# One low-part subtraction in four moved from VectorE to GpSimd in the experts' weight splits

## The chip, the cores and the metric

The program runs on one core of a Trainium2 chip. The metric is the device time of one execution in microseconds (us), the median of several runs. The engines are named as in the profile: PE is TensorE (PEld its weight loads), ACT is ScalarE, DVE is VectorE, POOL is GpSimd, SP is SyncE, which here only issues transfers.

## The reference

Three transformer blocks run one after another on 512 tokens of width 1024, all in float32. The change touches only the last part of the third block, a mixture of 32 experts. Cut to what matters:

```python
def hierarchical_moe(x, w_group, b_group, w_expert, b_expert, w_gate, w_up, w_down):
    # each token: best of 4 groups, then the best 2 of that group's 8 experts
    ...
    def run_block(args):
        xblk, e = args                       # up to 128 tokens of expert e
        hid = jax.nn.silu(xblk @ w_gate[e]) * (xblk @ w_up[e])
        return hid @ w_down[e]
    yb = lax.map(run_block, (xb, block_expert)).reshape(cap, d)
    y = yb * slot_w[:, None]
    ... # summed per token
```

`w_gate` and `w_up` are 1024x512 and `w_down` is 512x1024 for each expert, 2 MB each in float32.

## The kernel before

Every float32 product is made of three matmuls in the faster fp32r format. A weight tile `raw` is split in two: `h`, the value rounded to fp32r, and `l = raw - h`, the low part, rounded as well. With the activations split in the same way, the product is (high x high) + (high x low weight) + (low x high weight). The split is one ACT instruction (`copy`, profile line L184) and one DVE instruction (`tensor_sub`, L185), both of 128x1024 elements in the expert stage.

The expert stage is the last 600 us or so of the program. Each expert has 12 weight pieces of 128x1024 elements (512 KB): four of gate, four of up, four of down. SP loads them far ahead into 13 rotating `ew` buffers and, for every second expert, into the tiles `B` (gate), `hH` (up) and `A` (down). `splits` (from L1882) takes one piece, allocates a high and a low tile from two pools of three buffers each (`wh`, `wl`), and issues the cast and the subtraction. A piece then feeds six PE matmuls of 128x512: L2045 to L2047 for gate and up, L2073 to L2075 for down; the second of each three (L2046, L2074) is the one that reads `wl`. With three buffers the cast of a piece cannot start until PE has finished with the piece three places ahead of it.

The stages follow one another on PE in the order up(e+1), gate(e+2), down(e+1), up(e+2) and so on, four pieces each. Between them stand the transposes of the gathered tokens and of the hidden activations (L208), whose results `px` are split into `hL` or `dHL` by ACT and DVE again (L184, L185, 128x512). DVE also multiplies gate and up (L2062). POOL's queue holds two indirect transfers per expert: the gather of an expert's tokens (L2053, `C<-dr,itok`), which waits for PE's transposes of the tokens that the buffer held, and the scatter with addition of its result (L2078, `dr<-C,itok`), which waits for ACT's scaled copies of the result (L2077). Each engine executes its queue in order; the queues are laid out by a scheduler when the program is built. A loop for experts with more than 128 tokens stands behind the 32 experts.

Of the kernel before, what the change touches and what calls it, by code (L numbers as in the profile page):

```python
# [1300 lines left out]
def block3(K, out):  # L1301
    nc, tc, a = K.nc, K.tc, K.a
# [522 lines left out]
    def esrc(e):  # L1825
        return list(epieces(wG[e], wU[e], wD[e]))
# [3 lines left out]
    def eload(src, raw=None):  # L1830
        if raw is None:
            raw = ep.tile([P, 2, S], F32, name=K.nm("ew"), tag="ew")
        nc.sync.dma_start(raw, src)
        return raw
# [44 lines left out]
    for j, b in enumerate([st_[:, j] for j in range(4)] + [brow(), brow()]):  # L1879
        pre.append(eload(esrc(2)[j], b.rearrange("p (k n) -> p k n", k=2)))  # L1880

    def splits(raw):  # L1882
        h = K.wh.tile([P, 2, S], F32R, name=K.nm("wh"), tag="wh")
        l = K.wl.tile([P, 2, S], F32R, name=K.nm("wl"), tag="wl")
        K.split(h, l, raw)
        return h, l


    with ExitStack() as ctx:
# [9 lines left out]
        with ExitStack() as c2:  # L1899
# [106 lines left out]
            with tc.issue_after(last.ins):  # L2006
                for k in range(3):
                    pre[k] = splits(pre[k])
# [72 lines left out]
        def parts_of(pieces, ready=(), bufs=()):  # L2081
            ready, pieces, bufs = list(ready), list(pieces)[len(ready):], list(bufs)

            def nxt():
                r = ready.pop(0) if ready else eload(pieces.pop(0), bufs.pop(0) if bufs else None)
                return r if isinstance(r, tuple) else splits(r)

            return nxt
# [66 lines left out]
def whole(tc, a, out):  # L2155
    with ExitStack() as ctx:
        K_ = K(tc, ctx, a)
        block1(K_)
        block2(K_)
        block3(K_, out)  # L2160
# [32 lines left out]
```

## Time and profile before

| | |
|---|---|
| median of 3 runs | 2992.31 us (2991.24 to 2999.27) |
| the profiled execution: its time | 2999.19 us |
| its span, first to last instruction | 2997.3 us |
| PE busy over the span | 2883.6 us (96%) |
| DVE busy | 1754.3 us (59%) |
| ACT busy | 1410.7 us (47%) |
| POOL busy | 160.6 us (5%) |

Shares over the whole span mix stages with different limits. For this change only the stage from about 2340 us to 2965 us counts, and in it the question is which engine another one waits for, not which is busy. The stage repeats almost to the nanosecond from expert to expert: the scatter starts at 2521.97 us and the next at 2540.80 us, so one expert takes 18.83 us.

### The profile page before, as it was taken

To read this page: it belongs to the slowest core of one execution; us is meant where nothing else is said; L and a number is where in the kernel's file an instruction comes from. 1 tells how busy PE (TensorE), PEld (TensorE's weight loads), DVE (VectorE), ACT (ScalarE), POOL (GpSimd) and SP (SyncE) were. 2 spreads that over 40 slices of the span, in tenths; PEclk is the share of its full clock that TensorE was granted. 3 is DMA by queue.
4 is the path that set the end of the run, shared out by engine and by line. 5 is a ranking of instruction groups with operands and counts; after the bars stand their busy time and mean duration, and the time that the engine had idled before them with its cause. 6 is when DMAs were issued, how large, how long until landed. Compare 5 with 4: busy or idle time off the path is not lost.

```text
span 2997.3 us, 38485 instructions
## 1 busy us (share of the span) xinstructions
PE 2883.6 (96%) x14652; PEld 2377.1 (79%) x14652; DVE 1754.3 (59%) x2815; ACT 1410.7 (47%) x2297; POOL 160.6 (5%) x145
## 2 busy tenths in 40 slices
PE   8999999999999999999999999999999799999995
PEld 7788878888788878778888889888877577777774
DVE  4544453344675675645333363766554788888886
ACT  4422333333354455532222223656343488888885
POOL 0000000000000000000000000000000111111111
PEclk9999999999999999899999999999999799999998
DMA  5233333333422221133333343112433899999984
GB/s 174 90 93 92 96 95 98 99 98 94 122 70 56 66 57 47 46 120 99 99 99 95 105 132 115 29 36 73 157 117 144 292 318 347 338 344 365 353 309 141
DMA packets 330693, 428.42 MB, mean 143 GB/s; under 512 B 34381, under 2 KB 240904, under 8 KB 330506
## 3 DMA queue, kind: packets, MB, share of 16 engines
q1 hardware_dynamic: 320714, 415.41, 42.2%
q0 software_dynamic: 9792, 10.53, 1.6%
q8 instruction: 116, 1.90, 0.3%
q14 instruction: 71, 0.58, 0.1%
HBM read 420.60 MB, written 30.41 MB: 150 GB/s over the span
## 4 chain that ended last, share of the span: by engine, by line
PE 70%; issue 14%; DMA 8%; DVE 4%; ACT 2%; POOL 1%; POOLq 0%; SPq 0%; DVEq 0%; ACTq 0%
PE pf L267 28%; DMA dr<-C,itok 7%; PE pc L310 5%; PE pc L311 5%; PE pc L309 5%; PE pf L342 2%; PE pf L343 2%; PE pf L344 2%; PE pnO L1554 1%; PE pg L1650 1%; PE phO L1140 1%; PE pf L179 1%; PE pf L180 1%; PE pf L181 1%; PE pnS L179 1%
## 5 line engine op out<-in xcount | busy, mean ns | idle before, releaser
L159 DVE TENSOR_TENSOR wl<-raw,wh 128x1024 fp32r<-128x1024 f32 (+2 forms) x322 | 391.2, 1215 | 686.0 <-ACT wh L158 682.8
L158 ACT CAST wh<-raw 128x1024 fp32r<-128x1024 f32 (+2 forms) x322 | 336.3, 1045 | 865.1 <-PE pf L267 365.3
L267 PE MATMUL pf<-hL,wh 128*128 128x512 f32 x1272 | 501.7, 394 | 0.0
L267 PE MATMUL pf<-hH,wh 128*128 128x512 f32 x1208 | 478.2, 396 | 0.0
L267 PE MATMUL pf<-hH,wl 128*128 128x512 f32 x1208 | 476.1, 394 | 0.0
L267 PEld LDWEIGHTS pf<-hL,wh 128*128 128x128 f32 x1272 | 239.4, 188 | 51.2 <-issue 3.7
L267 PEld LDWEIGHTS pf<-hH,wh 128*128 128x128 f32 x1208 | 227.6, 188 | 52.3 <-issue 4.6
L267 PEld LDWEIGHTS pf<-hH,wl 128*128 128x128 f32 x1208 | 227.3, 188 | 48.8 <-issue 2.6
L185 DVE TENSOR_TENSOR wl<-ew,wh 128x1024 fp32r<-128x1024 f32 x186 | 225.9, 1223 | 34.0 <-ACT wh L184 29.8
L184 ACT CAST wh<-ew 128x1024 fp32r<-128x1024 f32 x186 | 194.2, 1053 | 48.5 <-PE pc L2047 31.0
L2046 PE MATMUL pc<-wl,hL 128*128 128x512 f32 x512 | 204.8, 400 | 0.5 <-DVE wl L185 0.4
L2047 PE MATMUL pc<-wh,hL 128*128 128x512 f32 x512 | 204.5, 400 | 0.0
L2045 PE MATMUL pc<-wh,hL 128*128 128x512 f32 x512 | 204.0, 399 | 0.0
L192 POOL TENSOR_TENSOR s<-s,mhalf 128x1 f32<-128x1 f32 (+1 forms) x69 | 57.8, 838 | 2253.3 <-DVE s L190 2244.6
L342 PE MATMUL pf<-wh,hH 128*128 128x256 f32 (+2 forms) x576 | 164.3, 286 | 0.0
L343 PE MATMUL pf<-wl,hH 128*128 128x256 f32 (+2 forms) x576 | 163.0, 283 | 0.0
L309 PE MATMUL pc<-wh,B 128*128 128x512 f32 x416 | 162.9, 392 | 0.0
L310 PE MATMUL pc<-wl,B 128*128 128x512 f32 x416 | 162.8, 391 | 0.0
L344 PE MATMUL pf<-wh,hL 128*128 128x256 f32 (+2 forms) x576 | 162.2, 282 | 0.0
L311 PE MATMUL pc<-wh,C 128*128 128x512 f32 x320 | 124.6, 389 | 0.0
L2046 PEld LDWEIGHTS pc<-wl,hL 128*128 128x128 f32 x512 | 96.3, 188 | 27.7 <-DVE wl L185 3.0
L2073 PE MATMUL pc<-wh,dHL 128*128 128x512 f32 x256 | 103.3, 404 | 11.1 <-ACT dHL L184 11.1
(695 smaller groups left out, 5932.3 us busy)
## 6 DMA issues: line engine op xcount, KB each, us to landing
raw<-w_in SPq DMA_DIRECT2D x111, 512.0 KB, 3.9
raw<-w_ff SPq DMA_DIRECT2D x64, 512.0 KB, 3.8
ew<-moe_w_down SPq DMA_DIRECT2D x64, 512.0 KB, 9.4
B<-moe_w_gate SPq DMA_DIRECT2D x64, 512.0 KB, 6.6
hH<-moe_w_up SPq DMA_DIRECT2D x64, 512.0 KB, 6.6
A<-moe_w_down SPq DMA_DIRECT2D x64, 512.0 KB, 6.3
ew<-moe_w_up SPq DMA_DIRECT2D x62, 512.0 KB, 5.5
ew<-moe_w_gate SPq DMA_DIRECT2D x60, 512.0 KB, 6.6
```

Of the source, the lines that this page charges most:

```text
L158: nc.scalar.copy(h, raw)
L159: nc.vector.tensor_sub(l, raw, h)
L185: self.nc.vector.tensor_sub(l, src, h)
L267: self.nc.tensor.matmul(ps[:n, sl], u[:, k], v[:, sl], start=(k == 0 and i == 0 and sl.start == 0), stop=(k == nk - 1 and i == 2), skip_gr ...
L309: mm(pss[t][:, :n], ah[:, ts], wh[:, k], start=(kg == 0), stop=False)
L310: mm(pss[t][:, :n], ah[:, ts], wl[:, k], start=False, stop=False)
L311: mm(pss[t][:, :n], al[:, ts], wh[:, k], start=False, stop=(kg == nk - 1))
L342: mm(o[t], ah[:, ts], wh[:, k], start=st, stop=False, skip_group_check=True)
L343: mm(o[t], ah[:, ts], wl[:, k], start=False, stop=False, skip_group_check=True)
L344: mm(o[t], al[:, ts], wh[:, k], start=False, stop=(kg == nk - 1), skip_group_check=True)
L2046: mm(ps, aH[:, kg], l[:, k], start=False, stop=False)
L2047: mm(ps, aL[:, kg], h[:, k], start=False, stop=(kg == n - 1))
```

## The change

The split of an expert's weight piece is written out in `splits`, with a counter. The cast stays on ACT. The subtraction of every fourth piece is issued to GpSimd instead of VectorE:

```diff
+    nsp = [0]
+
+
     def splits(raw):
+        nsp[0] += 1
         h = K.wh.tile([P, 2, S], F32R, name=K.nm("wh"), tag="wh")
         l = K.wl.tile([P, 2, S], F32R, name=K.nm("wl"), tag="wl")
-        K.split(h, l, raw)
+        nc.scalar.copy(h, raw)
+        (nc.vector if nsp[0] % 4 else nc.gpsimd).tensor_sub(l, raw, h)
         return h, l
```

Since each of gate, up and down has four pieces, it is always the fourth piece of each. Below L1881 the line numbers grow by five: L2046 becomes L2051, L2053 becomes L2058, L2078 becomes L2083, and the subtractions of the pieces stand at L1890.

On POOL, at the start of the expert stage, the queue before held three memsets, the gathers and the scatters:

```order
L1898 MEMSET C_18688 128x1024 x2
L1914 MEMSET C_18688 128x128
L2053 DMA C_18688<-dr_18207,itok 128x1024 x4
L2078 DMA dr_13402<-C_18688,itok 512x1024
L2053 DMA C_18688<-dr_18207,itok 128x1024
```

Now the subtractions stand among them:

```order
L1903 MEMSET C_18688 128x1024 x2
L1919 MEMSET C_18688 128x128
L2058 DMA C_18688<-dr_18207,itok 128x1024 x3
L1890 TENSOR_TENSOR wl_18865<-ew_18273,wh_18864 128x1024
L1890 TENSOR_TENSOR wl_18908<-ew_18341,wh_18907 128x1024
L2058 DMA C_18688<-dr_18207,itok 128x1024
L1890 TENSOR_TENSOR wl_18967<-B_18659,wh_18966 128x1024
L1890 TENSOR_TENSOR wl_19019<-ew_18421,wh_19018 128x1024
L2083 DMA dr_13402<-C_18688,itok 512x1024
L1890 TENSOR_TENSOR wl_19065<-hH_18664,wh_19064 128x1024
L2058 DMA C_18688<-dr_18207,itok 128x1024
```

From the last scatter on, the pattern repeats for each expert: scatter, the fourth up piece, a gather, the fourth gate piece, the fourth down piece, the next scatter. POOL gains 99 such instructions, three of them in the loop behind the experts.

On DVE, in the repeating part, with an even expert's up and down in `ew` and the next expert's gate in `B`, the queue before was:

```order
L185 TENSOR_TENSOR wl_19564<-ew_19561,wh_19563 128x1024
L185 TENSOR_TENSOR wl_19576<-ew_19573,wh_19575 128x1024
L185 TENSOR_TENSOR wl_19606<-B_18659,wh_19605 128x1024
L185 TENSOR_TENSOR wl_19617<-B_18659,wh_19616 128x1024
L2062 TENSOR_TENSOR scr_19475<-scr_19475,pc_19536 128x512
L185 TENSOR_TENSOR wl_19628<-B_18659,wh_19627 128x1024
L185 TENSOR_TENSOR hL_18689<-px_19596,hL_18689 128x512
L185 TENSOR_TENSOR wl_19639<-B_18659,wh_19638 128x1024
L185 TENSOR_TENSOR wl_19663<-ew_19660,wh_19662 128x1024
```

and now it is:

```order
L1890 TENSOR_TENSOR wl_19564<-ew_19561,wh_19563 128x1024
L1890 TENSOR_TENSOR wl_19606<-B_18659,wh_19605 128x1024
L1890 TENSOR_TENSOR wl_19617<-B_18659,wh_19616 128x1024
L2067 TENSOR_TENSOR scr_19475<-scr_19475,pc_19536 128x512
L1890 TENSOR_TENSOR wl_19628<-B_18659,wh_19627 128x1024
L185 TENSOR_TENSOR hL_18689<-px_19596,hL_18689 128x512
L1890 TENSOR_TENSOR wl_19663<-ew_19660,wh_19662 128x1024
```

`wl_19576` (fourth up piece) and `wl_19639` (fourth gate piece) are gone from DVE; what was behind each has moved up one place. PE's and ACT's queues are in the same order as before. On SP a few loads have changed places with their neighbours.

## Rows read from the trace of the kernel before

**Rows 1.** Stretches: PE, PEld, DVE, ACT, POOL busy (us), PEclk, DMA share, GB/s
```profile
2500.00:2600.00 100.00, 98.18 (x447) 79.82 (x446) 88.42 (x85) 82.96 (x97) 16.42 (x11) 1.00 0.95 340
2950.00:2960.00 10.00, 8.65 (x40) 6.96 (x40) 8.29 (x9) 6.55 (x8) 0.00 (x0) 1.00 0.00 1
```

**Rows 2.** Waits, 2400 to 2900 us: waiter, awaited: total us, times, longest
```profile
ACT wh L184 <- PE pc L2047: 50.2, 103, 0.8
...
ACT wh L184 <- PE pc L2075: 25.9, 81, 0.4
...
PE pc L2073 <- ACT dHL L184: 8.4, 23, 0.4
...
PEld pc L2046 <- DVE wl L185: 1.2, 8, 0.2
ACT wh L184 <- DMA hH<-moe_w_up: 0.8, 1, 0.8
```

**Rows 3.** Timeline of ACT: start, duration, instruction
```profile
2520.44 1.25 ACT L2077 ACTIVATE C<-pc,wsl 128x512 f32<-128x512 f32 x2
2521.59 1.99 ACT L184 CAST wh<-ew 128x1024 fp32r<-128x1024 f32 x2
...
2528.43 1.05 ACT L184 CAST wh<-B 128x1024 fp32r<-128x1024 f32 x1
...
2535.57 1.05 ACT L184 CAST wh<-ew 128x1024 fp32r<-128x1024 f32 x1 [0.31 <-PE pc L2075]
```

**Rows 4.** Timeline of PE: matmuls that first read a piece's low part
```profile
2520.86 0.39 PE L2046 MATMUL pc<-wl,hL 128*128 128x512 f32 x1
...
2525.45 0.39 PE L2046 MATMUL pc<-wl,hL 128*128 128x512 f32 x1
...
2531.38 0.40 PE L2046 MATMUL pc<-wl,hL 128*128 128x512 f32 x1
...
2534.21 0.40 PE L2074 MATMUL pc<-wl,dHL 128*128 128x512 f32 x1
...
2538.34 0.39 PE L2074 MATMUL pc<-wl,dHL 128*128 128x512 f32 x1
```

**Rows 5.** Timeline of DVE over the same expert
```profile
2522.66 2.36 DVE L185 TENSOR_TENSOR wl<-ew,wh 128x1024 fp32r<-128x1024 f32 x2 [0.87 <-ACT wh L184]
...
2528.24 1.22 DVE L185 TENSOR_TENSOR wl<-B,wh 128x1024 fp32r<-128x1024 f32 x1
...
2529.98 1.22 DVE L185 TENSOR_TENSOR wl<-B,wh 128x1024 fp32r<-128x1024 f32 x1
...
2536.65 1.23 DVE L185 TENSOR_TENSOR wl<-ew,wh 128x1024 fp32r<-128x1024 f32 x1
2538.04 2.59 DVE L185 TENSOR_TENSOR wl<-hH,wh 128x1024 fp32r<-128x1024 f32 x2 [0.16 <-ACT wh L184]
```

**Rows 6.** POOL's groups: count, busy us and mean ns, idle before
```profile
L2078 POOL DMA_INDIRECT dr<-C,itok x32 | 50.7, 1586 | 404.3 <-ACT C L2077 392.2 <-DVE wl L185 12.1
...
L192 POOL TENSOR_TENSOR s<-s,mhalf 128x1 f32<-128x1 f32 x56 | 43.7, 780 | 1970.1 <-DVE s L190 1961.3 <-DVE C L929 5.6 <-ACT C L1860 3.1
...
L1898 POOL MEMSET C<- 128x1024 f32 x2 | 1.8, 954 | 6.7 <-PE pf L1863 6.7
...
L1914 POOL MEMSET C<- 128x128 f32 x1 | 0.2, 210 | 0.0
```

**Rows 7.** Timeline of POOL in the expert stage
```profile
2521.97 1.59 POOL L2078 DMA_INDIRECT dr<-C,itok  x1 [12.16 <-ACT C L2077]
2527.27 1.38 POOL L2053 DMA_INDIRECT C<-dr,itok  x1 [3.71 <-PE px L208]
2540.80 1.59 POOL L2078 DMA_INDIRECT dr<-C,itok  x1 [12.16 <-ACT C L2077]
```

**Rows 8.** Timeline at the end of the program: DVE and POOL
```profile
2979.58 1.28 DVE L2149 SCALAR_TENSOR_TENSOR X<-X,mu,bc 128x1024 f32<-128x1024 f32 x1
2979.75 1.54 POOL L192 TENSOR_TENSOR s<-s,mhalf 128x1 f32<-128x1 f32 x1 [3.67 <-DVE s L190]
...
2983.12 1.28 DVE L2149 SCALAR_TENSOR_TENSOR X<-X,mu,bc 128x1024 f32<-128x1024 f32 x1
2983.29 1.52 POOL L192 TENSOR_TENSOR s<-s,mhalf 128x1 f32<-128x1 f32 x1 [2.00 <-DVE s L190]
```

**Rows 9.** The chain that ended last: start, us, what
```profile
2521.97 10.28 DMA dr<-C,itok
```

**Rows 10.** Waits of SP's queue, 2400 to 2900 us
```profile
SPq L1833 <- DVE wl L185: 360.9, 271, 3.4
```

## The prediction, made before the changed kernel was run

> **What bounds the kernel now.** I read the stretches first, since the page's shares mix stages. In a typical 100 us of the expert stage PE is busy 98.18 us at a granted clock of 1.00, DVE 88.42, ACT 82.96, POOL 16.42 [rows 1]. PE is the bound, and DVE is close behind it. Next I read who waits for whom: ACT's casts wait for PE to give a `wh` buffer back (50.2 and 25.9 us), while PE's own waits in 500 us are 8.4 us for the hidden activations and 1.2 us for low parts from DVE; the casts wait 0.8 us for a load [rows 2]. So nothing that DVE does costs PE more than 1.2 us today. The converse matters more: with three buffers the splits cannot run far ahead, and a split that gets slower is soon waited for. How soon is read from the timelines, at the fourth piece of up, gate and down of one expert [rows 3 to 5].
>
> **What the change removes.** Per expert DVE loses three subtractions of 1.22 us [rows 5], 3.7 us of its 16.7 us (88.42% of the 18.83 us from scatter to scatter [rows 7]). PE waited only 1.2 us in all for these, so the gain is at most that: 1.2 us over the stage.
>
> **What it adds.** Per expert POOL gets three subtractions of 128x1024. Call the duration of one T. No row of before shows POOL doing this, so I bound it. From below: DVE needs 1.22 us [rows 5]. POOL's memset, which only writes, takes 0.954 us for 1024 columns and 0.210 for 128 [rows 6], so 0.83 ns a column and about 0.10 us fixed. A subtraction reads two streams and writes one. If POOL needs two passes at that rate (the two reads in turn, the write beside them), T = 0.10 + 2 x 0.85 = 1.80 us; with three passes in turn T = 2.65 us. The powers of one column take 0.78 us [rows 6]; at such a rate for every column T would be hundreds of us, but a power is another kind of work than a subtraction, and I leave that end out. I take the middle of the two passes, T = 2.225 us, and keep 1.80 and 2.65 for the range. The Trainium skill (GPSIMD Engine Reference, section 3.1) gives 4497 ns for an addition of 2048 columns on GpSimd; half of it, 2.25 us, is an estimate by which the sum below would be 81 us. No run here shows that figure yet.
>
> **How much of T is hidden.** A fourth piece can start on POOL when its cast is done, plus a hand-over. DVE starts 0.03 us after a cast (end 2536.62, start 2536.65 [rows 3, 5]); POOL's scatter starts 0.28 us after ACT's copies (2521.69 to 2521.97 [rows 3, 7]); I take 0.2. From the end of a subtraction to PE's first matmul on it I also take 0.2: gate's fourth ends at 2531.20 and is read at 2531.38 [rows 4, 5]. The room for T is then:
> - up: the cast ends at 2523.58 (the second of the pair). DVE is in the third piece's subtraction until about 2523.85 (half of the pair from 2522.66). Letting POOL start behind it, room to 2525.45 - 0.2 is 1.40 us.
> - gate: cast end 2529.48, start 2529.68, room to 2531.18 is 1.50 us.
> - down: cast end 2536.62, start 2536.82, room to 2538.14 is 1.32 us.
>
> Together 4.22 us. What T has beyond its room is a stall of PE, and each stall counts in full: PE has no slack to catch up with, and the next casts wait for PE's buffers, so they move by the same amount. Per expert that is 3T - 4.22 = 6.68 - 4.22 = 2.46 us, and for 32 experts (the count of scatters [rows 6]; the loop behind them did not run, so 96 subtractions) 79 us. At T = 1.80 it is 1.18 us and 38 us in all; at 2.65 it is 3.73 and 119 us.
>
> **What is behind the moved instruction.** In POOL's queue each fourth up piece stands behind a scatter. That one runs from 2521.97 to 2523.56 [rows 7], just before the 2523.78 at which the piece could start; a stall moves both. The gather behind the up piece waits for PE anyway (from 2527.27 for 1.38 us [rows 7]) and is through before the gate piece is due; the tokens it fetches are wanted an expert later. SP waits for subtractions before it reloads a raw buffer (360.9 us [rows 10]); it will now sometimes wait for POOL, about 1 us longer, in front of other loads. These loads are for pieces far ahead, and the casts' wait of 0.8 us for loads [rows 2] says that there is room. The few loads that changed places on SP and the registers read at the end I cost at nothing for the same reason. Nothing in ACT's or PE's order moves.
>
> **A rule to weigh.** At the end of the program a one-column power on POOL, 0.78 us in the mean, takes 1.54 and 1.52 us where a DVE instruction with two wide inputs from the same memory is under way; it ends 0.43 and 0.41 us after DVE's [rows 6, 8]. So POOL seems to be held until DVE's instruction is over. The Trainium skill (SBUF — State Buffer, section "SBUF: two separate sides") says that GpSimd and a VectorE instruction with two SBUF inputs take a shared pair of ports by an exclusive lock, for the whole instruction, whoever starts first. The rows agree with it for POOL held by DVE; that DVE is held by POOL, no row of before shows. By that rule the sum would be the same if POOL finds the ports free, and larger as in the first rival if it does not. I have put the one hold that the timelines show (up) into the room already.
>
> Does DVE itself get late if it is held? After gate, POOL would be busy from 2529.68 to 2531.90; DVE's next two subtractions end at about 2533.1 and 2534.3, while PE wants the first of them at 2534.2 [rows 4] plus the stall of 0.7. After down, POOL ends at 2539.04; DVE's next (before at 2538.04 [rows 5]) ends at 2540.3. PE's first up piece, read at 2520.86 [rows 4], comes again 18.83 us later, at 2539.69; less the hand-over and plus the stall of 0.9 that is about 2540.4. That is just enough each time. So I cost it at nothing, with little to spare.
>
> **Against the clock.** With 2.46 us more per expert PE is busy 18.5 of 21.3 us, 87%. In a stretch with 8.65 of 10 us the granted clock was still 1.00 [rows 1], so I expect the upper level, 2.4 GHz, to hold.
>
> **The sum.** The profiled execution took 2999.2 us, so 3078 us by the rows; the median of the runs is 2992.3, 7 us lower, and I predict from it: 2992.3 + 79 = 3071 us.
>
> **Rivals.**
> 1. POOL and DVE hold each other at each hand-over. For: rows 8, and DVE's small margins above. Against: at gate and down DVE's subtraction is over before the cast is. Price: half a DVE subtraction, 0.61 us, on each of the three; 4.29 us per expert, 137 us, so 3129 us.
> 2. POOL's scatter keeps POOL occupied until its data lands (10.28 us [rows 9]) rather than for its 1.59 us. Then the fourth up piece starts at 2532.25 and comes 9 us late: 9.2 x 32 = 294 us, and 52 for the other two stalls, near 3340 us. Against: the record of the scatter ends long before its data lands.
> 3. Not slower: POOL is about as fast as DVE. The place is the same, the fourth pieces; it decides at T = 1.32 to 1.50 us, below which no stall is left. The gain is then at most 1.2 us: 2991 us. For: a memset takes 0.954 us [rows 6], less than DVE's subtraction. Against: a subtraction moves three streams where a memset moves one.
>
> **How the numbers follow.** The forecast, with T from about 1.7 to 2.75, gets 0.70; its own range is 2992 + 28 to 2992 + 129, so 3020 to 3121 us. Rival 1 gets 0.17, rival 2 0.03, rival 3 0.05; the remaining 0.05 is a T between 1.4 and 1.7, with 0 to 30 us of stall. The range from 3020 to 3140 holds the forecast and more than half of rival 1, about 8 in 10. A measurement of this kernel tells about 0.3%, 9 us, from no change. Rival 3 is within that, with a small part of the 0.05 of small stalls; faster by over 0.3% would need a gain of 9 us where at most 1.2 is to be had. So faster 0.01, same 0.06, slower 0.93.
>
> **What would show it.** Right: POOL's L1890 near 2.2 us, 96 of them; one expert taking about 21.3 us from scatter to scatter; PE's waits at L2051 and L2079 for `wl` put down to POOL, 0.7 to 0.9 us each, where 1.2 us in all stood before; DVE's share in the stage falling from 0.88 to about 0.61 (13.0 of 21.3 us); clock 1.00. Wrong: POOL's subtraction under 1.5 us and no waits of PE; DVE's subtractions growing from 1.22 us or PE waiting for DVE's pieces (rival 1); POOL's subtractions starting only when a scatter has landed (rival 2); or a granted clock below 1.00 between 2400 and 2900 us.

## The result, and the profile after

The changed kernel takes 3064.11 us (median of 4 runs, 3057.47 to 3073.74), the kernel before 2992.26; the ratio is 1.0237, with a 95% interval of 1.0205 to 1.0270. It is slower, by 72 us. Predicted were 3071 us, with a range of 3020 to 3140.

The first view is that of POOL's groups, which answers to [rows 6]: line, operation, shapes, count, busy time and mean ns of one.

```profile
L1890 POOL TENSOR_TENSOR wl<-ew,wh 128x1024 fp32r<-128x1024 f32 x47 | 112.8, 2399 | 120.1 <-issue 94.0 <-ACT wh L1889 16.2 <-DMA hH<-moe_w_up 9.6
...
L1890 POOL TENSOR_TENSOR wl<-hH,wh 128x1024 fp32r<-128x1024 f32 x16 | 38.6, 2412 | 6.4 <-ACT wh L1889 4.3 <-issue 2.0
L1890 POOL TENSOR_TENSOR wl<-B,wh 128x1024 fp32r<-128x1024 f32 x16 | 38.5, 2404 | 24.0 <-ACT wh L1889 18.0 <-DMA ew<-moe_w_up 6.0
L1890 POOL TENSOR_TENSOR wl<-A,wh 128x1024 fp32r<-128x1024 f32 x16 | 38.3, 2392 | 84.3 <-issue 78.8 <-ACT wh L1889 5.5
```

With one more piece in `X` that makes 96 subtractions of 2.4 us. Next the waits between 2400 and 2900 us, to be read against [rows 2]: waiter, awaited, total, times, longest.

```profile
PEld pc L2051 <- POOL wl L1890: 47.7, 47, 1.0
...
PE pc L2051 <- POOL wl L1890: 27.1, 47, 0.6
PEld pc L2079 <- POOL wl L1890: 26.1, 23, 1.1
...
PE pc L2079 <- POOL wl L1890: 16.3, 23, 0.7
```

PE now waits for POOL at each of the moved pieces, and in this list no wait of PE for a low part from DVE is left. SP's queue now waits for POOL as well (81.4 us in 35 waits, 3.3 at most), but no cast waits for a load in these 500 us. The stretch of the changed kernel, as in [rows 1]:

```profile
2500.00:2600.00 100.00, 89.25 (x393) 68.92 (x392) 76.87 (x61) 73.82 (x85) 48.53 (x25) 1.00 0.89 304
```

The granted clock stays at 1.00, 2.4 GHz. DVE falls only to 76.87%, which the subtractions taken from it do not explain; more on that below. Three timelines of one expert show the stalls. POOL first (start, duration, instruction, idle time before):

```profile
2541.43 2.39 POOL L1890 TENSOR_TENSOR wl<-ew,wh 128x1024 fp32r<-128x1024 f32 x1 [5.53 <-issue]
2546.30 1.59 POOL L2083 DMA_INDIRECT dr<-C,itok  x1 [2.48 <-ACT C L2082]
2548.05 2.42 POOL L1890 TENSOR_TENSOR wl<-hH,wh 128x1024 fp32r<-128x1024 f32 x1 [0.16 <-issue]
2552.46 1.13 POOL L2058 DMA_INDIRECT C<-dr,itok  x1 [2.00 <-PE px L208]
2554.82 2.39 POOL L1890 TENSOR_TENSOR wl<-ew,wh 128x1024 fp32r<-128x1024 f32 x1 [1.23 <-DMA hH<-moe_w_up]
```

The transfer named in the last row fills another tile than the piece reads; the piece's cast ends at 2554.67, 0.15 us before POOL starts, as at the other two pieces (0.13 and 0.15 us).

Then PE's timeline at the same three pieces (down, up, gate), the matmul before the low part and the one that reads it:

```profile
2542.76 0.39 PE L2078 MATMUL pc<-wh,dHL 128*128 128x512 f32 x1
2543.87 0.50 PE L2079 MATMUL pc<-wl,dHL 128*128 128x512 f32 x1 [0.72 <-POOL wl L1890]
...
2549.53 0.40 PE L2050 MATMUL pc<-wh,hL 128*128 128x512 f32 x1
2550.52 0.50 PE L2051 MATMUL pc<-wl,hL 128*128 128x512 f32 x1 [0.59 <-POOL wl L1890]
...
2556.30 0.40 PE L2050 MATMUL pc<-wh,hL 128*128 128x512 f32 x1
2557.26 0.50 PE L2051 MATMUL pc<-wl,hL 128*128 128x512 f32 x1 [0.57 <-POOL wl L1890]
```

Two neighbouring matmuls start 0.23 us apart when nothing is missing. Here they start 1.11, 0.99 and 0.96 us apart, so the stalls are 0.88, 0.76 and 0.73 us, 2.37 us per expert. Each matmul starts 0.05 us after POOL's subtraction ends. The matmul behind each starts 0.33 or 0.34 us later instead of 0.23, which this count leaves out; it gives each stall to about 0.1 us. And DVE's timeline:

```profile
2542.69 3.34 DVE L1890 TENSOR_TENSOR wl<-hH,wh 128x1024 fp32r<-128x1024 f32 x2 [1.39 <-ACT wh L1889]
2546.99 1.23 DVE L1890 TENSOR_TENSOR wl<-hH,wh 128x1024 fp32r<-128x1024 f32 x1 [0.96 <-ACT wh L1889]
2549.14 3.54 DVE L1890 TENSOR_TENSOR wl<-ew,wh 128x1024 fp32r<-128x1024 f32 x2 [0.92 <-ACT wh L1889]
...
2556.08 3.35 DVE L1890 TENSOR_TENSOR wl<-A,wh 128x1024 fp32r<-128x1024 f32 x2 [1.06 <-ACT wh L1889]
```

A pair of subtractions takes 2.4 to 2.6 us in [rows 5]; these pairs take 3.34, 3.54 and 3.35. Each begins while POOL is at work and is about 1 us longer: DVE is held, and the record of its instruction contains the hold. That is why DVE looks 76.87% busy.

To compare kernels apart from what the rest of the program does, I use the time from the first to the last scatter, read from POOL's timeline of each run: 2388.39 to 2967.47 us before, 579.1 us; 2373.53 to 3029.15 after, 655.6 us. The stage is 76.5 us longer; over its 31 intervals that is 2.47 us per expert. In this profiled execution the stage began 14.9 us earlier than in that of before, in a part of the program that is unchanged but ran at another mean granted clock (0.98 over the first 2300 us before, 0.99 after), and so the spans differ by only 62 us.

### The profile page after: what moved, and what is told of

Read it like the earlier page. It is cut to its first block, busy times and chain, and to the rows that moved or that the text cites. A ratio compares the mean times of both kernels' runs of the same rounds, so it can differ in the third digit from the quotient of the medians.

```text
span 3059.7 us, 38482 instructions
## 1 busy us (share of the span) xinstructions
PE 2886.4 (94%) x14652; PEld 2357.0 (77%) x14652; DVE 1736.5 (57%) x2719; ACT 1416.0 (46%) x2297; POOL 383.9 (13%) x241
## 5 line engine op out<-in xcount | busy, mean ns | idle before, releaser
L1890 DVE TENSOR_TENSOR wl<-ew,wh 128x1024 fp32r<-128x1024 f32 x139 | 212.2, 1553 | 74.5 <-ACT wh L1889 74.4
L2051 PE MATMUL pc<-wl,hL 128*128 128x512 f32 x512 | 211.3, 413 | 36.2 <-POOL wl L1890 36.1
L2051 PEld LDWEIGHTS pc<-wl,hL 128*128 128x128 f32 x512 | 96.5, 189 | 81.1 <-POOL wl L1890 64.1
L1890 POOL TENSOR_TENSOR wl<-ew,wh 128x1024 fp32r<-128x1024 f32 x47 | 112.8, 2399 | 120.1 <-issue 94.0
L2079 PE MATMUL pc<-wl,dHL 128*128 128x512 f32 x256 | 104.1, 406 | 22.8 <-POOL wl L1890 22.8
```

What stands on the lines that cost most here:

```text
L1890: (nc.vector if nsp[0] % 4 else nc.gpsimd).tensor_sub(l, raw, h)
L2051: mm(ps, aH[:, kg], l[:, k], start=False, stop=False)
```

## Experiments

Three theories were in play. *Room*: a low part from POOL comes late by what its 2.4 us exceed the time between its cast and PE's need. *Load*: VectorE and GpSimd exclude each other, and the sum of their work sets the length of an expert. *Hold*: each hold costs where it falls, if what it delays is due soon. Ratios are those to the kernel before, with 95% intervals; it was run again beside the others and took 2984.69 us beside the first four kernels below and 2987.16 beside the rest (half pieces, another piece, writes only, extra pairs spread evenly). "Stage" is the time from first to last scatter in the profiled execution (before: 579.1 us).

**One piece per expert.** Only gate's fourth piece goes to GpSimd.

```diff
-        (nc.vector if nsp[0] % 4 else nc.gpsimd).tensor_sub(l, raw, h)
+        (nc.gpsimd if nsp[0] % 12 == 0 or nsp[0] == 4 else nc.vector).tensor_sub(l, raw, h)
```

> Only the fourth piece of each gate goes to GpSimd (32 subtractions), the others stay on VectorE. Room theory (a piece's subtraction of 2.40 us is late for PE by what it has beyond the room that three buffers leave): one stall of about 0.73 us per expert as in the changed kernel's gate, 32 x 0.73 = 23 us above the kernel before, about 3016 us, the expert at 19.6 us. Load theory (the expert lasts as long as VectorE's and GpSimd's work in turn, since they exclude each other): 15.4 + 2.4 = 17.8 us is under the 18.83 us of PE, so no change, 2992 us.

Ratio 1.0054 (1.0031 to 1.0076), 3003.33 us, so about 16 us slower (9 to 23); stage 602.6 us, 23.5 us longer. POOL's timeline, from scatter to scatter:

```profile
2599.30 1.59 POOL L2083 DMA_INDIRECT dr<-C,itok  x1 [9.56 <-ACT C L2082]
...
2618.87 1.59 POOL L2083 DMA_INDIRECT dr<-C,itok  x1 [9.56 <-ACT C L2082]
```

The expert takes 19.57 us, 0.74 more than before, the size of the one stall. The room theory said 0.73 and 23 us, which the stage bears out; the medians give somewhat less. The load theory said nothing would happen; it fails here. One stall counts in full; that the three of the changed kernel, 2.37 us, come near its 2.47 us per expert fits stalls that simply add up.

**Room given to GpSimd's pieces, and its control.** Every fourth piece, in experts 2 to 30, takes its tiles from extra buffers (code shortened; the two `K` lines are those of before, indented):

```diff
+        if nsp[0] % 4 == 0 and 24 < nsp[0] <= 372:
+            if not xw:
+                xw.append(K.slot("X", [P, 4, D], F32R))
+            j = nsp[0] // 4 % 2 * 2
+            h, l = (xw[0][:, j + i].rearrange("p (k n) -> p k n", k=2) for i in range(2))
+        else:
+            h = K.wh.tile(...)
+            l = K.wl.tile(...)
```

> The changed kernel, but every fourth piece takes its high and low tile from an extra pair of buffers in a tile that is free at this time (experts 2 to 30), so that a piece's buffers come back after four pieces instead of three and the cast can start one piece, about 1.36 us, earlier. Room theory: room 2.7 to 2.9 us against 2.40, no stall is left, the expert back at about 18.9 us and the time at 2990 to 3005 us. Load theory: VectorE 13.7 us and GpSimd 7.2 us in turn are 20.9 us per expert, and no buffer changes that: about 3050 to 3065 us.

> The control for the extra pair of buffers: the same buffers, every subtraction on VectorE. Both theories: PE waited 1.2 us for low parts before, so no change within 0.3%, 2985 to 3000 us.

With GpSimd: ratio 1.0350 (1.0316 to 1.0384), 3093.24 us, slower than the changed kernel; stage 685.7 us. All on VectorE: ratio 0.9964 (0.9942 to 0.9985), 2977.88 us; stage 565.9 us. Neither theory had the first right, and the control, expected within 0.3% of before, came out a little faster. The edit gives more room than the expectation says: there are two extra pairs, taken in turn (`j` is 0 or 2), so a fourth piece's buffers come back after eight pieces, those of the other three after four. The fourth piece's cast is issued ahead of the other three of its group, in both kernels alike, so POOL's pieces come very early and PE never waits for them. PE's waits in the GpSimd version are these (2400 to 2900 us):

```profile
PE pc L2059 <- DVE wl L1898: 35.5, 42, 1.5
PE pc L2060 <- DVE hL L185: 16.7, 22, 2.0
```

They are for DVE. A DVE row of the same run shows three subtractions in 7.98 us, where three on their own take 3.7:

```profile
2610.86 7.98 DVE L1898 TENSOR_TENSOR wl<-ew,wh 128x1024 fp32r<-128x1024 f32 x3 [1.81 <-ACT wh L1897]
```

POOL's subtractions of 2610.31 (2.97 us) and 2615.30 (2.46 us) lie over it. The granted clock also fell to 0.96 in the mean over 2400 to 2900 us. The two stages differ by 119.8 us (the medians by 115). As an estimate from that mean, the clock cannot have taken more than 4% of the stage of 685.7 us, 27 us; some 90 us are left, more than the 76.5 of the changed kernel's stalls. So room was only the nearest limit: take it away, and the holds, behind which PE did not wait in the changed kernel, cost more than the stalls did.

**GpSimd working for nobody.** All low parts on VectorE; GpSimd subtracts into a tile that nobody reads, three times per expert (shown is the subtraction; the tile and the three calls are left out).

```diff
+            def pad(self, x):
+                nc.gpsimd.tensor_sub(dum, dum, x[:, 0:7].rearrange("p a b -> p (a b)"))
```

> The kernel before with all subtractions on VectorE; GpSimd makes three subtractions of 128x896 per expert (about 2.1 us each) into a tile that nobody reads, so nobody waits for them. If VectorE is not held by GpSimd: no change, 2992 us, VectorE's subtractions all 1.22 us. If the two exclude each other for whole instructions: VectorE has 16.7 us of its own and up to 6.3 us of holds in an expert of 18.83, so VectorE becomes the bound: 20.3 to 23 us per expert, 3040 to 3125 us, with many of VectorE's subtractions at 2 to 3.3 us.

Ratio 1.0486 (1.0448 to 1.0523), 3137.1 us; stage 720.3 us. The three subtractions run one behind the other. POOL and DVE at that place:

```profile
2617.33 9.04 POOL L2066 TENSOR_TENSOR dum<-dum,hL 128x896 f32<-128x896 f32 x3 [1.57 <-DVE hL L185]
```

```profile
2617.09 1.22 DVE L185 TENSOR_TENSOR wl<-B,wh 128x1024 fp32r<-128x1024 f32 x1
2618.22 6.18 DVE L185 TENSOR_TENSOR wl<-ew,wh 128x1024 fp32r<-128x1024 f32 x2
2624.33 0.68 DVE L185 TENSOR_TENSOR dHL<-px,dHL 128x512 fp32r<-128x512 f32 x1
```

POOL's take 3.01 us each, DVE's 3.09 instead of 1.22: this is what two engines look like that take turns, one instruction each, while both queues are full. No engine waits for POOL in the 500 us from 2400 to 2900 us. PE waits 56.4 us there for the split of the hidden activations (`dHL`), which stands behind the held pair, and the mean granted clock is 0.93. PE at such a wait, two experts later:

```profile
2667.90 0.40 PE L2083 MATMUL pc<-wl,dHL 128*128 128x512 f32 x1
2670.97 1.21 PE L2084 MATMUL pc<-wh,dHL 128*128 128x512 f32 x2 [2.68 <-DVE dHL L185]
2671.99 0.63 PE L2082 MATMUL pc<-wh,dHL 128*128 128x512 f32 x1
2672.41 0.63 PE L2083 MATMUL pc<-wl,dHL 128*128 128x512 f32 x1
```

Behind the wait the matmuls start 0.42 us apart instead of 0.23 until about 2674.5, and the granted clock is 0.57 in the mean from 2671 to 2675. Eight matmuls take 3.5 us instead of 1.8, so the clock costs about 1.7 us, on top of a wait of 2.7; the expert takes 23.58 us, 4.75 more than before. The slowdown is a little over the range that I gave (20.3 to 23 us per expert); without the 1.7 us of the clock, which I had not counted, it would lie inside it, by this estimate.

**The same time of GpSimd, hardly a read.** Each of these subtractions is replaced by one of a single column and three memsets.

```diff
-                nc.gpsimd.tensor_sub(dum, dum, x[:, 0:7].rearrange("p a b -> p (a b)"))
+                nc.gpsimd.tensor_sub(dum[:, 0:1], dum[:, 0:1], x[:, 0, 0:1])
+                for _ in range(3):
+                    nc.gpsimd.memset(dum, 0.0)
```

> As the run in which GpSimd worked for nobody, but its work is three memsets of 128x896 (about 0.85 us each, 2.5 us together) behind a subtraction of one column, three times per expert: as much time of GpSimd, with hardly a read. If it is GpSimd's reading that holds VectorE: no change, 2985 us within 0.3%, VectorE's subtractions at 1.22 us. If any instruction of GpSimd on the same memory holds VectorE: 3040 to 3140 us, as in the run with subtractions.

Ratio 1.0007 (0.9985 to 1.0029); stage 578.4 us. In 500 us POOL is busy 338.1, and DVE's group of subtractions is as before (1223 ns in the mean there):

```profile
L185 DVE TENSOR_TENSOR wl<-ew,wh 128x1024 fp32r<-128x1024 f32 x158 | 191.9, 1222 | 26.7 <-ACT wh L184 22.4
```

So POOL's wide subtractions, which read, hold DVE; its memsets, which only write, do not, for as much time of POOL and more. That is as the Trainium skill's page SBUF — State Buffer has it (section "SBUF: two separate sides"): a VectorE instruction with two SBUF inputs contends only with a GpSimd instruction that reads SBUF.

**Half pieces.** GpSimd and VectorE make 512 columns each of the fourth pieces.

```diff
-        (nc.vector if nsp[0] % 4 else nc.gpsimd).tensor_sub(l, raw, h)
+        if nsp[0] % 4:
+            nc.vector.tensor_sub(l, raw, h)
+        else:
+            nc.gpsimd.tensor_sub(l[:, 0], raw[:, 0], h[:, 0])
+            nc.vector.tensor_sub(l[:, 1], raw[:, 1], h[:, 1])
```

> The changed kernel, but GpSimd makes only the first 512 columns of the low part of every fourth piece, VectorE the other 512. From 2.40 us for 1024 columns and about 0.1 us fixed, GpSimd needs about 1.25 us. Room theory: rooms as measured in the changed kernel (duration less stall) are 1.5 to 1.7 us, so no piece is late and the expert is back at 18.83 us, 2985 us (within 0.3%). Hold theory (what costs is that the two engines exclude each other, wherever it falls): GpSimd's 3.75 us per expert still hold VectorE, and the half piece on VectorE comes behind GpSimd's, 0.65 us later than on its own: 0.2 to 0.5 us per piece, 3005 to 3030 us.

Ratio 1.0041 (1.0018 to 1.0064), 2997.47 us; stage 589.0 us, 9.9 longer. POOL at a down piece, held by DVE's half, and at a gate piece, not held:

```profile
2604.14 1.76 POOL L1893 TENSOR_TENSOR wl<-ew,wh 128x512 fp32r<-128x512 f32 x1 [5.98 <-issue]
...
2616.01 1.28 POOL L1893 TENSOR_TENSOR wl<-ew,wh 128x512 fp32r<-128x512 f32 x1 [0.83 <-DMA hH<-moe_w_up]
```

At 1.28 us for 512 columns nearly all the stall is gone, as room said; 0.3 us per expert are left (19.13 us against 18.83). PE's weight loads waited 13.2 us for POOL at the down pieces (26 times, 0.5 at most), where POOL came second, and PE's rows put the rest there:

```profile
2624.60 0.39 PE L2082 MATMUL pc<-wh,dHL 128*128 128x512 f32 x1
2625.07 0.50 PE L2083 MATMUL pc<-wl,dHL 128*128 128x512 f32 x1
2625.41 0.39 PE L2084 MATMUL pc<-wh,dHL 128*128 128x512 f32 x1
```

The starts lie 0.47 and 0.34 us apart instead of 0.23, 0.35 us in all: the piece is late because DVE holds POOL, which takes 1.75 us for it here. The room theory's no change is missed by a little (the interval begins at 1.0018); the hold theory was nearer in kind, and its 18 us and more too much.

**Another piece.** GpSimd makes the first piece of each down.

```diff
-        (nc.vector if nsp[0] % 4 else nc.gpsimd).tensor_sub(l, raw, h)
+        (nc.gpsimd if nsp[0] % 12 == 1 and nsp[0] > 12 else nc.vector).tensor_sub(l, raw, h)
```

> GpSimd makes the low part of the first piece of each down instead (one per expert); its cast ends at 2530.87 in the trace of before and PE reads it at 2534.21, so the room is 3.0 us against 2.40. Room theory without holds: no wait for GpSimd, no change, 2985 us. With holds: the second piece's subtraction on VectorE cannot start before GpSimd is through (about 2533.4), ends near 2534.6 instead of 2533.7, and the split of the hidden activations behind it ends about 0.7 us late; PE waits for that: 0.3 to 0.7 us per expert, 2994 to 3008 us.

Ratio 1.0042 (1.0020 to 1.0064), 2999.83 us; stage 590.9 us, 11.8 longer, 0.38 per expert. PE's weight loads do not wait for POOL once. They wait for the held DVE (2400 to 2900 us):

```profile
PEld pc L2080 <- DVE dHL L185: 14.3, 26, 0.8
PEld pc L2051 <- DVE wl L1890: 3.2, 21, 0.2
```

The hold itself, POOL's piece and the second piece's subtraction on DVE, which takes 1.22 us when free:

```profile
2611.03 2.47 POOL L1890 TENSOR_TENSOR wl<-A,wh 128x1024 fp32r<-128x1024 f32 x1 [2.32 <-issue]
```

```profile
2612.49 2.10 DVE L1890 TENSOR_TENSOR wl<-A,wh 128x1024 fp32r<-128x1024 f32 x1 [1.24 <-ACT wh L1889]
2614.51 0.68 DVE L185 TENSOR_TENSOR dHL<-px,dHL 128x512 fp32r<-128x512 f32 x1
```

This is the hold alone, at the place and of the size expected.

**The extra pairs spread evenly, all on VectorE.** Two of five pieces take the two extra pairs (`nsp[0] % 5 > 2` in place of `nsp[0] % 4 == 0`, and `j = (nsp[0] % 5 - 3) * 2`). There are five pairs of buffers in all, as in the control above; now every piece's come back after five pieces.

> All subtractions on VectorE, and two of every five pieces take the two extra pairs of buffers, so that a piece's buffers come back after five pieces. With one extra piece of room the expert went from 18.83 to 18.29 us. If what was gained is that casts no longer wait for PE's buffers, a further piece brings a little more: 18.1 to 18.3 us, 2965 to 2980 us. If PE's own order (transposes, the wait for the hidden activations) is all that is left: the same as with four, 2975 to 2980 us.

Ratio 0.9950 (0.9932 to 0.9968), 2966.96 us; stage 566.0 us, the same as in the control (565.9). So another piece of distance for the three in four gains nothing; more than five pairs were not tried. The two versions' intervals overlap; both lie below 1, and so below the kernel before and the changed one.

## Why the prediction was right

**Bound and sign.** PE was the bound, a piece that came late was waited for, and no gain was to be had from a lighter DVE. All of it held: PE's low-part waits grew from 1.2 us [rows 2] to a wait at every moved piece, and the run with one piece per expert showed that a stall counts in full.

**T.** Taken as 2.225 us, measured 2.40. Per expert that is 3 x 0.175 = 0.53 us too little. The true value lies between the two and the three passes that bounded it. The estimate from the Trainium skill's GPSIMD Engine Reference, 2.25 us, was 0.15 us short as well.

**Room.** Taken as 1.40, 1.50 and 1.32 us, 4.22 in all. Measured as duration less stall: 2.42 - 0.76, 2.39 - 0.73 and 2.39 - 0.88, or 1.66, 1.66 and 1.51 us, 4.83 in all. I gave 0.2 us to each hand-over; the cast that ends at 2541.30 is followed by POOL at 2541.43, and POOL's end at 2543.82 by PE at 2543.87. That is 0.18 to 0.2 instead of 0.4 us at gate and down, and instead of 0.47 at up, where I let POOL start behind DVE. The hold that I counted at up was hardly there: POOL starts at 2548.05 while DVE runs until 2548.22, and its record is only 0.03 us longer than at gate.

**The sum.** The two errors, 0.53 us of T and 0.61 us of room, nearly cancel: 2.37 us by the stalls and 2.47 by the stage, against 2.46 predicted. The mechanism was right; that the total came out closer than its terms is luck, since nothing ties the two errors to each other.

**Holds.** I costed DVE's being held at nothing, with little to spare. In the changed kernel that is right: DVE's pairs grow by about 1 us, and PE waits for none of them; as I read the timelines, its stall for POOL gives DVE the time, which the prediction had counted in its margins. It is right only there. Rival 1, holds at each hand-over at 3129 us, did not decide here, but its mechanism exists in both directions (DVE's pairs here, POOL's 1.76 us in the half pieces) and decides in three of the other kernels: extra buffers with GpSimd, GpSimd for nobody, another piece. Rival 2 (POOL occupied until the scatter's data lands) is excluded: the subtraction at 2548.05 starts 0.16 us after the scatter's record ends. Rival 3 needed T under 1.32 to 1.50 us.

**DVE's share and the clock.** I expected DVE's share at 0.61 and saw 0.77, because a held instruction counts as busy. The clock held at 1.00, as forecast.

## What to carry to other kernels

Before a step is moved to a slower engine, read from the timeline how long its consumer leaves it, piece by piece; the price is its duration less that room, and only on the engine that bounds. In these runs VectorE and GpSimd were not two engines for subtractions of two wide operands in SBUF, the memory that holds the tiles: they took turns where they met, so GpSimd's help cost VectorE about as much time as it saved (about 3 us of holds per expert against 3.7 us taken off), while memsets on GpSimd cost VectorE nothing. The two versions with extra buffers and no GpSimd are the only ones that were faster than before (0.9964 and 0.9950).

## What the runs showed of the hardware that I had not expected

- With both queues full the rows look as if GpSimd and VectorE alternate instruction by instruction, 3.01 and 3.09 us each, and the record of the held one contains the wait. A busy share of DVE beside a reading GpSimd is no measure of its work: 76.87% here, of which about 3 us per expert are holds.
- Extra buffers with all work on VectorE made the stage 13 us shorter, though PE's list of waits showed only 1.2 us for low parts; I had expected no change. In the repeating part an expert takes 18.29 us instead of 18.83. The buffers are not all that changed: the scheduler laid out PE's queue in another order. Before, PE's transposes (L208) break into the products at four places of an expert (from 2617.76, 2620.78, 2624.24 and 2626.72 us in one of them), with the extra buffers at two (from 2608.83 and 2614.77 us), in all three versions that have them. By the starts of PE's rows the two places that are gone cost 0.23 and 0.15 us, some 0.4 of the 0.54 us. So it may be the order rather than the room that gained; no run tells the two apart.
- The mean granted clock fell to 0.96 and 0.93 in the two runs in which PE had single waits of 2 us and more, and stayed at 1.00 in the changed kernel with three stalls of under 0.9 us per expert.
